# Fourteen second-pass pairs by seven products, every second one, all units kept in DRAM in two parts

## The chip, the cores and the metric

The kernel runs on one core of a Trainium2 chip. The metric is the device time of one execution in microseconds; lower is better. TensorE is called PE here, VectorE DVE, ScalarE ACT, GpSimd POOL and SyncE SP, as in the profile.

## The reference, cut to what matters

Two layers of a decoder trunk on 256 tokens of width 2048, all in float32:

```python
for l in range(2):
    h = rmsnorm(x, attn_norm_g[l])
    proj = h @ w_in[l]                       # 2048 -> 6144
    ...                                      # attention on one half, gated short conv on the other
    x = x + concat([attn, conv]) @ w_out[l]
    hm = rmsnorm(x, mlp_norm_g[l]) @ w_up[l]           # 2048 -> 8192
    x = x + square(relu(hm)) @ w_down[l]               # 8192 -> 2048
```

The change is in the last two lines, the MLP. `square(relu(hm))` is called the hidden units; `w_down` has 8192 rows and 2048 columns.

## The kernel before, in words

**Precision.** Every float32 operand is cut into two parts of a rounded float32 type: the high part is made by ACT (a copy that rounds), the low part by DVE (operand minus high part). A product of two such operands is three matmuls (high by high, high by low, low by high: `TERMS`). For PE a matmul of 128x128 by 128x512 is the unit of work.

**The MLP, `mlp` (L767).** The 8192 hidden units are taken in 32 pairs (`NP`) of two blocks of 128. There are two passes over the pairs.

- The *first pass* (L1015 to L1055) makes the hidden units of pair i by `w_up` (L961) and multiplies those of pair i-2 with the left 1024 columns of `w_down` by a scheme of seven products in place of eight (L1011). For that it needs, beside the four blocks of the units, four sums of them (S1 to S4, L984 to L987), and sums of the weights.
- The *second pass* (L1114 to L1177) multiplies the units with the right 1024 columns of `w_down`. It cannot make the units again, so the first pass has written them to DRAM, and the second pass loads them back. A pair in the tuple `SEVEN` (L36) is done by seven products, 7 x 3 = 21 matmuls (L1117 to L1134); any other pair (`PLAIN`) is done directly, 2 x 4 x 3 = 24 matmuls (L1169 to L1175).

Between the two passes PE does the left columns of pairs 30 and 31 directly (48 matmuls, L1090, called the left rest below). Their units are the last two users of the two `f` buffers.

**What the second pass loads of the units.** Plain pairs come in blocks of two (`block`, L1059): tile `g`, two DMAs of 512 KB on POOL's queue from the DRAM tile `plain`; there are four buffers. Pairs in `SEVEN` are of two kinds. Those in `WHOLE` (every second one) were written as finished forms in two parts (`both`, 896 KB) and are loaded straight into an `f` tile by a DMA on POOL's queue (L907). The others were written as raw units (`hid`, 448 KB), are loaded by a DMA on SP's queue into an `h` tile (L910), and ACT and DVE make the two parts (`rounded`, L1000, 128x896 each). `f` has two buffers, for both passes; a load into one waits until PE has done with what was in it.

**What sets the order.** PE's order is that of the code. `weights.take` makes the forms of weights three jobs ahead, in the order `made_in` (L931 to L945), which places the four jobs of a `SEVEN` pair (three kinds of weight forms and the loading of its units) beside jobs of the plain pairs ahead of it. The other engines' orders are set by a scheduler when the program is built; each engine and each DMA queue then runs its list strictly in order. `w_down` is loaded by SP, 1024 KB for each pair and pass: `draw` tiles for `SEVEN` pairs, `raw` for plain ones (L814).

**In this case.** `SEVEN` is (4, 6, 8, 10, 12, 15, 17, ..., 29), 13 pairs; 6, 10, 15, 19, 23 and 27 are `WHOLE`. The second pass starts with plain pairs 0 to 3, then does pair 4.

Of the kernel before, what the change touches and what calls it, by code (L numbers as in the profile page):

```python
# [9 lines left out]
F32 = mybir.dt.float32  # L10
F32R = mybir.dt.float32r
# [4 lines left out]
P = 128  # L16
# [16 lines left out]
AHEAD = 3  # L33
NP = DFF // (2 * P)
LAG = 2
SEVEN = (4, 6, 8, 10, 12, 15, 17, 19, 21, 23, 25, 27, 29)  # L36
WHOLE = SEVEN[1::2]
PLAIN = tuple(i for i in range(NP) if i not in SEVEN)

OUT_JOBS = D // P // 2 * (D // CH)  # L40
# [68 lines left out]
def trunk(ctx: ExitStack, tc: tile.TileContext, x, w_in, w_out, conv_w, q_norm_g, k_norm_g,  # L109
          lambda_q1, lambda_k1, lambda_q2, lambda_k2, subln_g, attn_norm_g, mlp_norm_g,  # L110
          w_up, w_down, rel_bias, selector, out):
    nc = tc.nc
# [7 lines left out]
    dram = ctx.enter_context(tc.tile_pool(name="dram", bufs=1, space=bass.MemoryType.DRAM))  # L120
# [8 lines left out]
    def behind(*instructions):  # L129

        stack = ExitStack()
        for ins in instructions:
            stack.enter_context(tc.issue_after(ins.ins))
        return stack
# [632 lines left out]
    def mlp(l, mnorm, ahead, last):  # L767
# [3 lines left out]
        with ExitStack() as scope:  # L771
            upool = scope.enter_context(tc.tile_pool(name="upool", bufs=3))
            fpool = scope.enter_context(tc.tile_pool(name="fpool", bufs=2))
            second = scope.enter_context(tc.tile_pool(name="second", bufs=1))
# [3 lines left out]
            def tile_of(tag, shape, dtype, *rooms):  # L778
                n = turn[tag] = turn.get(tag, -1) + 1
                pool, tag_in = rooms[max(n - (tag == "draw"), 0) % len(rooms)]  # L780
                return pool.tile(shape, dtype, tag=tag_in, name=tag, bufs=1)
# [27 lines left out]
            def load_rows(i, col):  # L809
                raw = (upool.tile([P, 2, 2 * CH], F32, tag="uraw", name="raw") if col and i not in SEVEN else  # L810
                       tile_of("draw", [P, 2, 2 * CH], F32, (first, "draw"), (second, "draw1"),
                               (second, "draw2")))
                with behind(*after_load(None if col else EARLY_DOWN.get(i))):
                    nc.sync.dma_start(  # L814
                        raw, w_down[l][i * 2 * P:(i + 1) * 2 * P, col:col + 2 * CH].rearrange(
                            "(k p) c -> p k c", p=P))
                return raw

            def quarters(i, col=0):


                keep = late if i == SEVEN[0] and col else lambda ins: None

# [65 lines left out]
            for i in range(NP - LAG, NP):  # L889
# [3 lines left out]

            hid = {i: dram.tile([P, 7 * P], F32, name=f"hid{l}_{i}") for i in SEVEN
                   if i not in WHOLE}
            both = {i: dram.tile([P, 2, 7, P], F32R, name=f"both{l}_{i}") for i in WHOLE}
            plain = [dram.tile([P, 2, 2, 4, P], F32R, name=f"plain{l}_{b}")
                     for b in range((len(PLAIN) + 1) // 2)]  # L900
            again, g_loads = {}, []

            def load_again(i):
                if i in WHOLE:
                    f = again[i] = fpool.tile([P, 2, 8, P], F32R, tag="f", name="f")
                    with behind(*g_loads[-1:]):
                        nc.gpsimd.dma_start(f[:, :, 1:], both[i])  # L907
                    return
                again[i] = tile_of("h", [P, 8, P], F32, (fpool, "h"), (second, "h"))
                nc.sync.dma_start(again[i][:, 1:].rearrange("p a c -> p (a c)"), hid[i])  # L910

            def unit(i):
                def make():
                    f = again[i] if i in WHOLE else rounded(again[i], 1, 8)
                    later = SEVEN.index(i) + 1
                    if later < len(SEVEN):
                        load_again(SEVEN[later])
                    return f
                return make
# [12 lines left out]
            mine = [where[i] + k for i in PLAIN for k in range(2)]  # L932
            slots = {}
            for i in SEVEN:
                before = [j for j in mine if j < where[i]][-4:] if i != SEVEN[0] else [
                    mine[0], mine[2], mine[5], mine[6]]
                js = [where[i] + k for k in (1, 2, 0, 3)]
                if len(before) == 4 and SEVEN.index(i) and where[SEVEN[SEVEN.index(i) - 1]] > before[0]:
                    before = [before[2], before[2], before[3], before[3]]
                for j, b in zip(js, before):  # L940
                    slots.setdefault(b, []).append(j)
# [32 lines left out]
            def square(i, h):  # L974


                u = h[:, 0:4].rearrange("p a c -> p (a c)")
                nc.scalar.activation(u, u, AF.Relu)
                top = h[:, 0:4].rearrange("p (k t) c -> p k t c", t=2)[:, :, 0]
                nc.vector.tensor_mul(top, top,  # L980
                                     mnorm.ratio.unsqueeze(1).to_broadcast([P, 2, P]))
                nc.scalar.activation(u, u, AF.Square)
                if i < NP - LAG:
                    nc.vector.tensor_add(h[:, S1], h[:, A21], h[:, A22])  # L984
                    nc.vector.tensor_sub(h[:, S2], h[:, S1], h[:, A11])
                    nc.vector.tensor_sub(h[:, S3], h[:, A11], h[:, A21])
                    nc.vector.tensor_sub(h[:, S4], h[:, A12], h[:, S2])  # L987
                if i in hid:
                    nc.gpsimd.dma_start(hid[i], h[:, 1:].rearrange("p a c -> p (a c)"))
                if i in SEVEN:  # L990
                    f = rounded(h, 1, 8)
                    if i in WHOLE:
                        nc.gpsimd.dma_start(both[i], f[:, :, 1:])
                    return f
                f = rounded(h, 0, 8 if i < NP - LAG else 4)
                b = PLAIN.index(i)
                stored.append(nc.gpsimd.dma_start(plain[b // 2][:, b % 2], f[:, :, :4]))
                return f

            def rounded(h, lo, hi):  # L1000
                f = fpool.tile([P, 2, 8, P], F32R, tag="f", name="f")
                nc.scalar.activation(f[:, 0, lo:hi], h[:, lo:hi], AF.Copy)
                nc.vector.tensor_sub(f[:, 1, lo:hi], h[:, lo:hi], f[:, 0, lo:hi].bitcast(F32))
                return f
# [10 lines left out]
            for i in range(NP):  # L1015
                j = i - LAG
                end = i == NP - 1
                h = tile_of("h", [P, 8, P], F32, (fpool, "h"), (second, "h"))
                if i == 0:
                    two = [mm.tile([P, 2, CH], F32, tag="mm2", name=f"up{c}")[:, 0].rearrange(  # L1020
                        "p (h s) -> p h s", h=2) for c in range(2)]
                    for kh in range(2):
                        for c in range(2):
                            up_part(two[c], kh)
                            if kh:
                                evict(two[c], h[:, 2 * c:2 * c + 2])
                    fs[0] = square(0, h)
                    continue
# [85 lines left out]
            for i in range(NP):  # L1114
                if i in SEVEN:
                    f = weights.take()
# [34 lines left out]
                if slot == 1 and b == 0:  # L1151
                    load_again(SEVEN[0])
                if i == PLAIN[-1]:
                    both = [weights.take() for k in range(2)]
# [34 lines left out]
    for l in range(DEPTH):  # L1189
        mnorm, ahead = mixer(l, norm, first_loads if l == 0 else lambda weights: None)  # L1190
        norm = mlp(l, mnorm, ahead, l == DEPTH - 1)
# [32 lines left out]
```

## Time and profile before

| what | value |
|---|---|
| time, median of 3 runs | 2140.8 us (2140.31 to 2140.87) |
| the profiled execution | 2139.43 us |
| its span, first to last instruction | 2137.7 us |
| DVE busy | 1689.8 us (79%) |
| ACT busy | 1292.7 us (60%) |
| moved by DMA | 487.79 MB, mean 228 GB/s |
| SP's queue (q1) | 413.40 MB |
| POOL's queue (q0) | 72.51 MB |
| second pass, layer 0 / layer 1 | from 906.4 us / from 1967.6 us |

The profiled execution is 1.4 us below the median of the runs, and lies 1.7 us over its span. A row of groups reads: line, engine, operation, out<-in by the program's names, shape, count, then busy us, mean ns of one, and idle time before it. Matmuls overlap each other, so the duration of one (389 ns) is not the time that PE spends for each; that is read from how long a run of them takes. DMA rows tell when a DMA was issued; "to landing" is the time from there until its data was in place.

### The profile page before, as it was taken

How to read it: one execution, taken by the hardware profiler on the slowest of the kernel's cores; microseconds unless marked ns; L12 is line 12 of the kernel's file. 1: busy time of each engine (PE TensorE's matmuls, PEld its weight loads, DVE VectorE, ACT ScalarE, POOL GpSimd, SP SyncE). 2: the span in 40 equal slices, each digit the busy share in tenths (PEclk: the TensorE clock that was granted, in tenths of full speed). 3: DMA queues.
4: the chain of work that ended last, by engine and by line, in shares of the span. 5: the costliest groups of instructions: out<-in, count | busy, mean ns of one | idle time of the engine just before them, and what ended most of it. 6: DMA issues, size and time to landing. Idle time of an engine off the chain costs nothing.

```text
span 2137.7 us, 28947 instructions
## 1 busy us (share of the span) xinstructions
PE 2127.5 (100%) x10956; PEld 1809.3 (85%) x10956; DVE 1689.8 (79%) x2307; ACT 1292.7 (60%) x1761; POOL 174.8 (8%) x263
## 2 busy tenths in 40 slices
PE   9999999999999999999999999999999999999999
PEld 7888888888888888888888888888888888888887
DVE  6677656788888888799866776567888888887987
ACT  6566445566666666655565664456666666665553
POOL 1021200000000000100001221000000000001000
PEclk9999999999999999999999999999999999999999
DMA  7655568577777777899466556776777777778992
GB/s 258 188 160 166 183 205 264 182 237 235 233 235 234 241 237 235 258 389 317 150 207 178 160 164 188 219 242 201 226 239 241 227 239 242 232 239 277 392 316 93
DMA packets 291701, 487.79 MB, mean 228 GB/s; under 512 B 10689, under 2 KB 191592, under 8 KB 291560
## 3 DMA queue, kind: packets, MB, share of 16 engines
q1 hardware_dynamic: 266936, 413.40, 61.0%
q0 software_dynamic: 24576, 72.51, 10.2%
q8 instruction: 86, 1.41, 0.3%
q14 instruction: 55, 0.45, 0.1%
q10 hardware_dynamic: 48, 0.02, 0.0%
HBM read 446.42 MB, written 39.48 MB: 227 GB/s over the span
## 4 chain that ended last, share of the span: by engine, by line
PE 97%; DVE 1%; DMA 1%; ACT 0%; issue 0%; SPq 0%; ACTq 0%
PE upc L961 31%; PE pr L1011 14%; PE rt L1173 9%; PE o L397 8%; PE rt L1011 6%; PE ci L419 4%; PE gc L419 4%; PE gb L419 4%; PE v L397 4%; PE k L397 4%; PE q L397 4%; PE upw L961 1%; PE pr L1090 1%; PE up L961 1%; PE sc L595 1%; PE av L634 0%
## 5 line engine op out<-in xcount | busy, mean ns | idle before, releaser
L310 ACT ACTIVATE whi<-raw 128x1024 fp32r<-128x1024 f32 x324 | 343.1, 1060 | 430.6 <-PE rt L1173 104.0
L311 DVE TENSOR_TENSOR wlo<-raw,whi 128x1024 fp32r<-128x1024 f32 x324 | 398.2, 1230 | 244.0 <-ACT whi L310 238.9
L961 PE MATMUL upc<-nT,uhi 128*128 128x512 f32 x1920 | 477.5, 391 | 0.0
L804 ACT ACTIVATE uhi<-uraw 128x1024 fp32r<-128x1024 f32 x256 | 270.5, 1057 | 266.2 <-PE upc L961 239.5
L805 DVE TENSOR_TENSOR ulo<-uraw,uhi 128x1024 fp32r<-128x1024 f32 x256 | 313.1, 1223 | 126.4 <-ACT uhi L804 114.9
L961 PEld LDWEIGHTS upc<-nT,uhi 128*128 128x128 f32 x1920 | 352.8, 188 | 68.1
L961 PEld LDWEIGHTS upc<-nT,ulo 128*128 128x128 f32 x1920 | 261.9, 190 | 18.7
L961 PE MATMUL upc<-nT,ulo 128*128 128x256 f32 x1920 | 267.7, 282 | 0.0
L1173 PE MATMUL rt<-whi,g 128*128 128x512 f32 x576 | 182.1, 389 | 0.0
L397 PE MATMUL o<-whi,cat 128*128 128x512 f32 x512 | 159.5, 390 | 0.0
L1173 PEld LDWEIGHTS rt<-whi,g 128*128 128x128 f32 x576 | 108.2, 188 | 22.3
L397 PEld LDWEIGHTS o<-whi,cat 128*128 128x128 f32 x512 | 96.1, 188 | 19.7
L1173 PE MATMUL rt<-wlo,g 128*128 128x512 f32 x288 | 112.2, 389 | 0.0
L829 DVE TENSOR_TENSOR t13l<-t,t13h 128x1024 fp32r<-128x1024 f32 x86 | 105.1, 1222 | 2.5
L829 DVE TENSOR_TENSOR b2l<-draw,b2h 128x1024 fp32r<-128x1024 f32 x86 | 104.7, 1217 | 0.8 <-ACT b2h L828 0.8
L829 DVE TENSOR_TENSOR t24l<-t,t24h 128x1024 fp32r<-128x1024 f32 x86 | 104.7, 1217 | 0.5 <-ACT t24h L828 0.5
L842 DVE TENSOR_TENSOR t<-draw 128x1024 f32<-128x1024 f32 x86 | 104.8, 1219 | 0.3
L397 PE MATMUL o<-wlo,cat 128*128 128x512 f32 x256 | 99.6, 389 | 0.0
L828 ACT ACTIVATE t13h<-t 128x1024 fp32r<-128x1024 f32 x86 | 91.4, 1063 | 4.3 <-PE rt L1011 1.8
L1011 PE MATMUL pr<-t13h,f 128*128 128x512 f32 x240 | 93.8, 391 | 0.0
L828 ACT ACTIVATE b2h<-draw 128x1024 fp32r<-128x1024 f32 x86 | 90.4, 1051 | 3.4 <-PE rt L1011 2.6
L828 ACT ACTIVATE t24h<-t 128x1024 fp32r<-128x1024 f32 x86 | 90.5, 1052 | 3.3 <-DVE t L846 3.3
(359 smaller groups left out, 3857.4 us busy)
## 6 DMA issues: line engine op xcount, KB each, us to landing
uraw<-in_w_up_dram SPq DMA_DIRECT2D x128, 1024.0 KB, 5.6
raw<-in_w_in_dram SPq DMA_DIRECT2D x190, 512.0 KB, 3.9
draw<-in_w_down_dram SPq DMA_DIRECT2D x90, 1024.0 KB, 7.4
raw<-in_w_down_dram SPq DMA_DIRECT2D x38, 1024.0 KB, 6.6
raw<-in_w_out_dram SPq DMA_DIRECT2D x64, 512.0 KB, 5.4
plain<-f POOLq DMA_DIRECT2D x38, 512.0 KB, 3.7
g<-plain POOLq DMA_DIRECT2D x38, 512.0 KB, 9.3
both<-f POOLq DMA_DIRECT2D x12, 896.0 KB, 4.4
```

The costliest lines, as they stand in the source:

```text
L310: self.splits.append((nc.scalar.activation(hi, raw, AF.Copy), nc.vector.tensor_sub(lo, raw, hi.bitcast(F32))))
L311: nc.vector.tensor_sub(lo, raw, hi.bitcast(F32))))
L397: nc.tensor.matmul(acc[:, t], a.ap[:, pa, k % KG, t * P:(t + 1) * P], (hi, lo)[pw][:, j], start=(k == 0 and n == 0), stop=(k == nk - 1 and ...
L419: nc.tensor.matmul(acc[:, f, 0] if part else acc[:, f], wt[:, k % 4, fs], a.ap[:, 0, k % KG] if part else a.ap[:, :, k % KG], start=(part ...
L804: nc.scalar.activation(hi, src, AF.Copy)
L805: nc.vector.tensor_sub(lo, src, hi.bitcast(F32))
L828: keep(nc.scalar.activation(hi, src, AF.Copy))
L829: keep(nc.vector.tensor_sub(lo, src, hi.bitcast(F32)))
L842: keep(nc.vector.tensor_sub(t[:, 0:2], raw[:, :, 1], raw[:, 0]))
L961: nc.tensor.matmul(acc[:, 0] if part else acc, wt[:, k], a.ap[:, 0, k % KG] if part else a.ap[:, :, k % KG], start=(part == 0 and kh == 0 ...
L1011: nc.tensor.matmul(prods[n], f[:, pa, a], b[pw], start=(start and m == 0), stop=(stop and m == 2))
L1173: nc.tensor.matmul(prods[p], blocks[b][:, slot, pa, 2 * k + t], w[pw][:, n], start=(i == PLAIN[0] and k == 0 and m == 0), stop=False)
```

## The change

`SEVEN` becomes every second pair from 3 to 29, 14 pairs; so plain pairs are 0, 1, 2, 4, 6, ..., 28, 30, 31, 18 in place of 19. `WHOLE` goes: all `SEVEN` pairs are written as forms in two parts (896 KB) and loaded straight into `f` by POOL's queue. The raw units in DRAM (`hid`), their load on SP's queue and the second `rounded` are gone. The jobs of the first `SEVEN` pair are placed beside other plain jobs, since only three plain pairs are ahead of it.

```diff
-SEVEN = (4, 6, 8, 10, 12, 15, 17, 19, 21, 23, 25, 27, 29)
-WHOLE = SEVEN[1::2]
+SEVEN = tuple(range(3, NP - 2, 2))
...
-            hid = {i: dram.tile([P, 7 * P], F32, name=f"hid{l}_{i}") for i in SEVEN
-                   if i not in WHOLE}
-            both = {i: dram.tile([P, 2, 7, P], F32R, name=f"both{l}_{i}") for i in WHOLE}
+            whole = {i: dram.tile([P, 2, 7, P], F32R, name=f"whole{l}_{i}") for i in SEVEN}
...
             def load_again(i):
-                if i in WHOLE:
-                    f = again[i] = fpool.tile([P, 2, 8, P], F32R, tag="f", name="f")
-                    with behind(*g_loads[-1:]):
-                        nc.gpsimd.dma_start(f[:, :, 1:], both[i])
-                    return
-                again[i] = tile_of("h", [P, 8, P], F32, (fpool, "h"), (second, "h"))
-                nc.sync.dma_start(again[i][:, 1:].rearrange("p a c -> p (a c)"), hid[i])
+                f = again[i] = fpool.tile([P, 2, 8, P], F32R, tag="f", name="f")
+                with behind(*g_loads[-1:]):
+                    nc.gpsimd.dma_start(f[:, :, 1:], whole[i])
 
             def unit(i):
                 def make():
-                    f = again[i] if i in WHOLE else rounded(again[i], 1, 8)
+                    f = again[i]
...
                 before = [j for j in mine if j < where[i]][-4:] if i != SEVEN[0] else [
-                    mine[0], mine[2], mine[5], mine[6]]
+                    mine[0], mine[1], mine[3], mine[4]]
...
-                if i in hid:
-                    nc.gpsimd.dma_start(hid[i], h[:, 1:].rearrange("p a c -> p (a c)"))
                 if i in SEVEN:
                     f = rounded(h, 1, 8)
-                    if i in WHOLE:
-                        nc.gpsimd.dma_start(both[i], f[:, :, 1:])
+                    nc.gpsimd.dma_start(whole[i], f[:, :, 1:])
                     return f
```

The first place is POOL's list at the end of the first pass and the start of the second, layer 0, before. `plain0_9` is the store of pair 31's units, the `g` rows are the blocks of plain pairs (x2: two DMAs), the `f` rows the units of a `SEVEN` pair, whose number stands behind `both0_`.

```order
L1062 DMA g_8427<-plain0_0_3766 128x1024 x2
L997 DMA plain0_9_3775<-f_8408 128x2x512
L1062 DMA g_8520<-plain0_1_3767 128x1024 x2
L1062 DMA g_8565<-plain0_2_3768 128x1024 x2
L1062 DMA g_8643<-plain0_3_3769 128x1024 x2
L907 DMA f_8595<-both0_6_3760 128x2x896
L1062 DMA g_8801<-plain0_4_3770 128x1024 x2
L1062 DMA g_8967<-plain0_5_3771 128x1024 x2
L907 DMA f_8823<-both0_10_3761 128x2x896
```

The same place of the change; `whole0_3` are the units of pair 3.

```order
L1052 DMA g_8427<-plain0_0_3767 128x1024 x2
L987 DMA plain0_8_3775<-f_8408 128x2x512
L1052 DMA g_8520<-plain0_1_3768 128x1024 x2
L1052 DMA g_8565<-plain0_2_3769 128x1024 x2
L1052 DMA g_8681<-plain0_3_3770 128x1024 x2
L903 DMA f_8568<-whole0_3_3753 128x2x896
L903 DMA f_8570<-whole0_5_3754 128x2x896
L1052 DMA g_8844<-plain0_4_3771 128x1024 x2
L903 DMA f_8700<-whole0_7_3755 128x2x896
```

The first `f` load stands at the same place in the list, behind one store and the six `g` DMAs of blocks 1 to 3; it is for pair 3 now, where it was for pair 6. Layer 1 reads the same.

The second place is SP's list at the same time, before: `w_down` and the raw units.

```order
L814 DMA raw_8456<-in_w_down_dram 128x2x1024
L814 DMA draw_8474<-in_w_down_dram 128x2x1024
L814 DMA raw_8523<-in_w_down_dram 128x2x1024
L814 DMA raw_8570<-in_w_down_dram 128x2x1024
L910 DMA h_8568<-hid0_4_3753 128x896
L814 DMA draw_8668<-in_w_down_dram 128x2x1024
L910 DMA h_8737<-hid0_8_3754 128x896
L814 DMA draw_8761<-in_w_down_dram 128x2x1024
L910 DMA h_8903<-hid0_12_3755 128x896
L814 DMA raw_8609<-in_w_down_dram 128x2x1024
```

And the change at this place:

```order
L813 DMA raw_8456<-in_w_down_dram 128x2x1024
L813 DMA draw_8474<-in_w_down_dram 128x2x1024
L813 DMA raw_8543<-in_w_down_dram 128x2x1024
L813 DMA raw_8572<-in_w_down_dram 128x2x1024
L813 DMA draw_8628<-in_w_down_dram 128x2x1024
L813 DMA draw_8724<-in_w_down_dram 128x2x1024
L813 DMA raw_8610<-in_w_down_dram 128x2x1024
L813 DMA raw_8706<-in_w_down_dram 128x2x1024
L813 DMA draw_8804<-in_w_down_dram 128x2x1024
```

The three loads of raw units (448 KB each) are gone from between the weights; the loads of weights stand in the same order otherwise (three `raw`, one `draw` among them, then two `draw`, then the fourth `raw`, which is that of pair 3 before and of pair 4 now).

The third place is PE, where pair 3 stands in layer 0. Before, after the last matmul of pair 2:

```order
L1173 MATMUL rt08_8519<-wlo_8589,g_8520 128x512
L1173 MATMUL rt08_8519<-whi_8588,g_8520 128x512
L1173 MATMUL rt02_8516<-whi_8611,g_8520 128x512
L1173 MATMUL rt02_8516<-wlo_8612,g_8520 128x512
L1173 MATMUL rt02_8516<-whi_8611,g_8520 128x512
```

And now:

```order
L1163 MATMUL rt08_8519<-wlo_8607,g_8520 128x512
L1163 MATMUL rt08_8519<-whi_8606,g_8520 128x512
L1001 MATMUL rt01_8658<-b1h_8476,f_8568 128x512
L1001 MATMUL rt01_8658<-b1l_8477,f_8568 128x512
L1001 MATMUL rt01_8658<-b1h_8476,f_8568 128x512
```

Right behind pair 2, where PE went on with `g`, it now reads `f_8568`, the tile that the first `f` load on POOL's queue fills.

## The prediction

> **What bounds the kernel now.** I read the page first (busy shares, the chain that ended last), then PE's waits, then the chain and the DMA rows of the second pass.
>
> ```profile
> PE 2127.5 (100%) x10956; PEld 1809.3 (85%) x10956; DVE 1689.8 (79%) x2307; ACT 1292.7 (60%) x1761; POOL 174.8 (8%) x263
> PE 97%; DVE 1%; DMA 1%; ACT 0%; issue 0%; SPq 0%; ACTq 0%
> PE up L961 <- DVE nT L277: 2.5, 4, 0.7
> PE q L397 <- DVE wlo L331: 1.5, 2, 1.3
> ```
>
> PE is the bound: it is busy in all but 10 us of the span, the chain is PE for 97%, and its two longest sums of waits are 2.5 and 1.5 us, neither of them in a second pass. So a matmul less is time gained, work taken from DVE or ACT gains nothing, and a new wait of PE costs its full length. The chain in the second pass, of layer 0 and then of layer 1:
>
> ```profile
> 895.63 10.88 PE pr L1090 x48
> 906.51 21.76 PE rt L1173 x96
> 928.27 4.76 PE rt L1011 x21
> 933.03 5.44 PE rt L1173 x24
> ```
> ```profile
> 1967.79 21.89 PE rt L1173 x96
> 1989.69 4.76 PE rt L1011 x21
> ```
>
> The columns are start, duration, matmuls. 96 matmuls take 21.76 us, so one costs PE 0.2267 us. Pairs 0 to 3 are those 96; the first pair by seven products, pair 4, begins at 928.27. Pair 3 therefore begins at 928.27 - 5.44 = 922.8 in layer 0 and at 1967.79 + 72 x 0.2267 = 1984.1 in layer 1. These are the moments when the changed PE first needs a loaded `f`.
>
> What serves it is POOL's queue. Its issues in layer 0, then the one `f` load in layer 1, and how long after their issue the six `g` loads (first) and the `f` loads (layer 0, layer 1) landed:
>
> ```profile
> 899.67 0.71 POOL L997 DMA_DIRECT2D plain<-f  x1 [7.96 <-DVE f L1003]
> 900.38 3.20 POOL L1062 DMA_DIRECT2D g<-plain  x6
> 906.81 0.71 POOL L907 DMA_DIRECT2D f<-both  x1 [3.23 <-PE pr L1090]
> 917.70 1.07 POOL L1062 DMA_DIRECT2D g<-plain  x2 [10.18 <-PE rt L1173]
> ...
> 1968.09 0.71 POOL L907 DMA_DIRECT2D f<-both  x1 [3.22 <-PE pr L1090]
> ```
> ```profile
> DMA to landing us min/median/max: 8.2/13.4/19.9
> DMA to landing us min/median/max: 20.9/20.9/20.9
> DMA to landing us min/median/max: 21.1/21.1/21.1
> ```
>
> The `f` load landed at 906.81 + 20.9 = 927.7 in layer 0 and at 1968.09 + 21.1 = 1989.2 in layer 1. The last of the six `g` loads was issued at about 903.0 and landed 19.9 later, at 922.9; the `f` load came 4.8 us behind it. So the queue is served in order, and this load waits for what stands ahead of it, not for its own issue. How fast the queue moves:
>
> ```profile
> 898.00:902.00 4.00, 4.00 (x19) 3.34 (x18) 3.20 (x5) 2.71 (x4) 2.33 (x5) 1.00 0.39 94
> 902.00:908.00 6.00, 6.00 (x28) 4.95 (x28) 5.80 (x7) 4.49 (x6) 2.29 (x4) 1.00 1.07 346
> 908.00:926.00 18.00, 18.00 (x81) 14.93 (x80) 14.69 (x16) 8.29 (x9) 1.07 (x2) 1.00 1.08 401
> ```
> ```profile
> q1 hardware_dynamic: 966, 3.63, 53.8%
> q0 software_dynamic: 997, 3.57, 53.5%
> ```
>
> The last three columns of the windows are the granted clock, the DMA share and GB/s: from 908 to 926 the DMA engines are full at 401 GB/s. In that window SP's queue (q1) moved 3.63 MB and POOL's (q0) 3.57 MB: each gets half, 200 GB/s, as long as both have work.
>
> **The change part by part.**
>
> *Six matmuls less.* Fourteen pairs in place of 13 take 21 matmuls in place of 24; that is 3 for each layer, 6 in all, 6 x 0.2267 = 1.36 us gained on PE.
>
> *The units of pair 3.* In the changed order POOL's first `f` load is for pair 3 and stands behind the same store and the same six `g` loads. Its buffer is free sooner (it takes that of pair 30, used until the middle of the left rest, 895.63 + 5.4 = 901), so it is issued at about 903.5 and not 906.8, but it lands when the queue has served what is ahead. If the queue moves as before, that is 927.7 and 1989.2, and PE, which needs it at 922.8 and 1984.1, waits 4.9 and 5.1 us: 10.0 us. Everything on PE stands behind it, since its order is fixed. What can make it shorter is less traffic on SP's queue:
>
> ```profile
> 899.40 0.34 SPq L910 DMA_DIRECT2D h<-hid  x1
> 900.74 0.37 SPq L814 DMA_DIRECT2D draw<-in_w_down_dram  x1
> 906.19 0.34 SPq L910 DMA_DIRECT2D h<-hid  x1
> 907.99 9.75 SPq L814 DMA_DIRECT2D raw<-in_w_down_dram  x3
> ```
> ```profile
> h<-hid SPq DMA_DIRECT2D x14, 448.0 KB, 4.3
> f<-both POOLq DMA_DIRECT2D x12, 896.0 KB, 8.1
> ```
>
> The two `hid` loads go, 2 x 0.459 = 0.92 MB, which took 0.92 / 0.401 = 2.3 us of full DMA. If SP's queue then stood empty for as long, POOL's load would land 2.3 us sooner and the waits would be 2.6 and 2.8 us, 5.4 in all. If the weight loads behind close up, nothing is won and it stays at 10.0. They can close up only in part: the next `draw` is issued at 900.74 and needs about 5 to 6 us at half rate, to some 907; the fourth `raw` waits for DVE to be done with the first one (907.99 before, perhaps 1.5 us sooner without the rounding of pair 4's units), and the window from 898 to 902 (94 GB/s, though DMAs were issued from 899.4 on) shows that a DMA moves little for a microsecond or two after its issue. I take an empty queue of about 1 us in each layer, nearer to closing up: waits of 3.9 and 4.1 us, **8.0 us**.
>
> *What is late next.* Pair 5's `f` is next in the queue: 0.92 MB at 200 GB/s, 4.6 us behind pair 3's, against the 10.2 us (4.76 + 5.44) that PE is busy before it needs it. Pair 7's is issued when PE has done pair 3, behind two `g` loads (1.05 MB, 5.2 us); it lands some 10 us behind pair 5's at the latest, about 15 us after pair 3 starts, and is needed 20.4 us after. From there each `f` load may start when the `SEVEN` pair two before is done, and is needed 5.44 + 4.76 + 5.44 = 15.6 us later; such loads landed after 8.1 us (median). So only pair 3 waits. If this cover failed, each us late would cost 26 us (13 pairs, two layers).
>
> *DVE and ACT.* DVE's groups in the second pass of layer 0:
>
> ```profile
> L311 DVE TENSOR_TENSOR wlo<-raw,whi 128x1024 fp32r<-128x1024 f32 x36 | 43.9, 1222 | 14.9 <-ACT whi L310 14.6
> L829 DVE TENSOR_TENSOR t24l<-t,t24h 128x1024 fp32r<-128x1024 f32 x13 | 15.8, 1218 | 0.0
> L846 DVE TENSOR_TENSOR t<-draw,t 128x512 f32<-128x512 f32 x13 | 8.9, 688 | 0.2
> L1003 DVE TENSOR_TENSOR f<-h,f 128x896 fp32r<-128x896 f32 x7 | 7.6, 1084 | 0.0
> ```
>
> A plain pair costs DVE 2 x 1.22 = 2.4 us, a `SEVEN` pair four such operations of 1.22 and three of 0.69, 6.9 us. One pair more by seven adds 4.5 us for each layer, the seven roundings gone take 7.6 us off. DVE has less to do, and PE waited for none of it worth naming: nothing either way. The forms of pair 3's weights come early enough, because their loads stand where those of pair 4 stood, while PE needs them 5.4 us sooner and DVE has the rounding less. If that failed, it would hide inside the wait for `f`.
>
> *The first pass.* Seven raw stores of 448 KB become 896 KB, and one plain store of 512 KB does, in each layer: 0.46 MB, or 1.1 us of full DMA, in pairs that take about 16 us.
>
> ```profile
> 423.00:443.00 20.00, 20.00 (x105) 17.16 (x104) 17.70 (x26) 14.70 (x19) 0.72 (x1) 1.00 0.84 261
> both<-f POOLq DMA_DIRECT2D x12, 896.0 KB, 4.4
> ```
>
> The DMA engines are 0.84 busy there, and the twelve pairs that already store 896 KB made PE wait for nothing. Zero; 8 x 1.1 us for each layer if that spare time were gone.
>
> *Sum.* Profiled execution 2139.43 - 1.36 + 8.0 = 2146.1. It lies 1.4 us below the median of the runs, so on that scale **2147.4 us**, 0.3% slower. This measurement can tell about 0.2%, 4.3 us, from no change. Ends of the unknown wait (5.4 and 10.0): 2144.8 and 2149.4.
>
> [...] In every window quoted the granted clock is 1.00, and PE's longest wait is 1.3 us, so the trace shows no long stop and what follows one. [...]
>
> [...]
>
> **The rivals.**
>
> 1. *PE's clock falls in the stop.* The price from rows: at half clock a `SEVEN` pair of 4.76 us takes 4.76 us more; half a pair slowed in each layer is 2 x 2.4 = 4.8 us on top, 2152.2; a whole pair each, 2157. For it: the waits of about 4 us are longer than anything in the trace. Against: nothing in the trace.
> 2. *Not slower: pair 3's `f` lands in time.* This decides if the load lands before 922.8. With SP's queue idle, the 0.52 + 6 x 0.52 + 0.92 = 4.6 MB would need 11.4 us at 401 GB/s and be there by 914. For it: `f` loads later in the pass land in 8.1 us. Against: SP's list still has four weight loads there, and six `g` loads land ahead in both layers. Then 2140.8 - 1.4 = 2139.4.
> 3. *Every `f` load is late.* All of them compete on POOL's queue now, 0.92 + 0.52 MB in 10.2 us, 141 GB/s, under its half of 200. One us late each: 2147 + 26 = 2173. Against: the 15.6 us above.
> 4. *The change does not do what it says.* PE's list holds exactly six matmuls less, so no.
>
> **How the numbers follow.** Forecast (a wait before pair 3 in both layers, clock kept) 0.62; rival 1 0.20; rival 2 0.12; rival 3 and other mishaps 0.06. The range leaves out rival 2 (0.12), rival 3 and the upper end of rival 1: 2142.5 to 2153.5; its lower end lets each wait be about 1 us under the bound of 2.6 to 2.8. Faster by over 0.2%, under 2136.5, has no mechanism: 0.02. Within 0.2%: rival 2 and the low end of the forecast, 0.19. Slower: 0.79.
>
> **What would show it.** In the trace after: PE idle before the first matmul with `f` behind pair 2, about 4 us, in both layers, ended by the DMA `f<-whole`; that load landing near 926.7 and 1988.2; no PE idle before pairs 5, 7 and later; 0.2267 us for each matmul after the wait (rival 1: 0.45 for a few us, and a granted clock under 1). PE without any idle there would make the prediction wrong, as would a wait for DVE instead of the DMA.

## The result, and the profile after

The changed kernel takes 2147.4 us (median of 6 runs, 2146.22 to 2150.45) against 2140.84 us (6 runs, 2139.36 to 2141.69): ratio 1.0033 [1.0021, 1.0046], slower. The profiled execution took 2148.12 us, its span is 2146.3 us, 8.6 us more than before.

The page after, busy times and the chain that ended last:

```profile
PE 2129.6 (99%) x10950; PEld 1810.0 (84%) x10950; DVE 1690.8 (79%) x2303; ACT 1287.1 (60%) x1751; POOL 186.5 (9%) x277
PE 94%; DMA 3%; DVE 1%; issue 1%; ACT 0%; POOL 0%; SPq 0%; ACTq 0%; POOLq 0%
```

PE runs the six matmuls less, and yet it is busy for 2.1 us more, so some of its matmuls have become slower. DMA, 1% of the chain before, is 3%. The longest sums of PE's waits after (us in total, times, longest):

```profile
PE rt L1001 <- DMA f<-whole: 4.6, 2, 2.3
PE up L954 <- DVE nT L276: 2.6, 4, 0.7
PE rt L1148 <- DVE x L1057: 2.3, 1, 2.3
```

The first is the forecast wait for pair 3's `f`, in both layers, but 2.3 us each and not 4. The third stands at the end of layer 0; the same wait before:

```profile
PE rt L1158 <- DVE x L1067: 0.4, 1, 0.4
```

Where the 8.6 us arise is seen in the chain of after, in both layers (start, duration, matmuls):

```profile
903.46 21.62 DMA f<-whole
...
925.12 5.07 PE rt L1001 x21
930.20 5.44 PE rt L1163 x24
...
1062.82 8.20 DMA raw<-in_w_in_dram
...
1071.13 1.07 ACT whi L309
...
1072.22 0.76 DVE wlo L310
...
1073.36 0.76 DVE x L1057
...
1074.16 4.60 PE rt L1148 x12
...
1080.51 4.55 PE q L396 x20
...
1970.31 21.55 DMA f<-whole
...
1991.90 6.66 PE rt L1001 x21
1998.57 5.44 PE rt L1163 x24
```

The end of layer 0 in the chain before:

```profile
1070.28 3.02 PE rt L1158 x12
...
1075.05 9.99 PE q L397 x44
```

Setting the same moments of the two chains side by side gives an account of the difference:

| moment | before | after | later by | new since the moment above |
|---|---|---|---|---|
| pair 3 done, layer 0 | 928.27 | 930.20 | 1.93 | -0.68 (three matmuls), 2.6 (wait for `f` and restart) |
| first matmul after the stop at the end of layer 0 | 1070.28 | 1074.16 | 3.88 | 1.95 (wait 2.3 in place of 0.4) |
| first `q` of layer 1 | 1075.05 | 1080.51 | 5.46 | 1.58 (12 matmuls in 4.60, not 3.02) |
| pair 3 done, layer 1 | 1989.69 | 1998.57 | 8.88 | -0.68, 4.1 (wait for `f`, then 6.66 for 21 matmuls, not 5.07) |
| span | 2137.7 | 2146.3 | 8.6 | -0.3 |

What makes the 12 and the 21 matmuls slow is the granted clock. The windows of after; the third number from the end is the clock, then DMA share and GB/s:

```profile
898.00:902.00 4.00, 4.00 (x20) 3.30 (x19) 3.15 (x5) 2.71 (x4) 2.38 (x5) 1.00 0.43 141
...
908.00:926.00 18.00, 15.66 (x70) 12.65 (x69) 15.00 (x16) 7.33 (x7) 1.10 (x2) 1.00 1.08 403
...
925.00:928.40 3.40, 3.28 (x14) 2.73 (x15) 1.36 (x2) 2.28 (x3) 0.00 (x0) 1.00 1.09 406
...
1074.30:1077.70 3.40, 3.40 (x9) 2.63 (x10) 1.95 (x4) 1.33 (x4) 0.00 (x0) 0.50 0.97 358
1992.50:1995.90 3.40, 3.40 (x10) 2.66 (x9) 1.89 (x2) 1.82 (x3) 0.00 (x0) 0.50 1.08 407
1996.00:1999.00 3.00, 3.00 (x15) 2.46 (x14) 1.90 (x2) 2.48 (x3) 0.12 (x1) 1.00 1.08 403
```

After the stop at the layer's end and after the one in layer 1, PE runs at half clock for 3.4 us, then at full clock again. After the equally long stop in layer 0, at 925, it keeps its clock. The clock record of the trace shows a difference between them: the two slow stretches begin at 1074.32 and 1992.51 and last 3.413 us each, and their beginnings lie 269 times this length apart. Counted back in steps of 3.413 us, this grid has lines at 1989.10, 1070.91, 924.14 and 920.73. Each of the two stops that cost the clock lies within one step, with 2.3 us of idle PE in it; the stop in layer 0, from 922.78 to 925.12, is parted by the line at 924.14 into 1.4 and 0.98 us.

The loads that the two kinds of stop go back to, first `g` and `f`. The landing times of the six `g` loads, and of pair 3's `f` (the same in both layers):

```profile
DMA to landing us min/median/max: 7.0/12.8/17.3
DMA to landing us min/median/max: 21.6/21.6/21.6
```

POOL's first loads, and SP's list at the same time:

```profile
900.32 3.20 POOL L1052 DMA_DIRECT2D g<-plain  x6
903.46 0.71 POOL L903 DMA_DIRECT2D f<-whole  x1
...
900.69 0.37 SPq L813 DMA_DIRECT2D draw<-in_w_down_dram  x1
906.28 6.41 SPq L813 DMA_DIRECT2D raw<-in_w_down_dram  x2
```

POOL issues its first six `g` at the same time as before (900.3, 900.4 before), yet the last lands after 17.3 us and not 19.9, and `f` at 903.46 + 21.6 = 925.1, 2.6 us sooner than the 927.7 of before. The store and the first `g` no longer meet a `hid` load: from 898 to 902 the DMA engines move 141 GB/s, 94 before. SP issues nothing between the `draw` at 900.69 and the next `raw` at 906.28, which came at 907.99 before.

At the end of layer 0 the two loads of layer 1's bias (`rev`, 1024 KB each, POOL) meet the first weights (`raw`, SP). After:

```profile
1062.03 1.81 POOL L261 DMA_DIRECT2D rev<-by_dist_d  x2 [18.62 <-PE rt L1001]
...
1062.82 11.02 SPq L349 DMA_DIRECT2D raw<-in_w_in_dram  x5
```

Before:

```profile
1061.18 1.82 POOL L262 DMA_DIRECT2D rev<-by_dist_d  x2 [29.88 <-PE rt L1011]
...
1060.90 9.05 SPq L350 DMA_DIRECT2D raw<-in_w_in_dram  x5
```

Before, the weights were 0.3 us ahead; after, the bias is 0.8 us ahead, and the weights on the chain need 8.2 us. ACT rounds them at 1071.13, DVE makes their low part, and behind that on DVE's list stands the operation on `x` (L1057) for which PE waits: the fourth to seventh rows of the chain above.

### The profile page after: what moved, and what is told of

The parts are those of the page before. It is cut to its first block, busy times and chain, and to the rows that moved or that the text cites. A ratio compares the mean times of both kernels' runs of the same rounds, so it can differ in the third digit from the quotient of the medians.

```text
span 2146.3 us, 28874 instructions
## 1 busy us (share of the span) xinstructions
PE 2129.6 (99%) x10950; PEld 1810.0 (84%) x10950; DVE 1690.8 (79%) x2303; ACT 1287.1 (60%) x1751; POOL 186.5 (9%) x277
## 4 chain that ended last, share of the span: by engine, by line
PE 94%; DMA 3%; DVE 1%; issue 1%; ACT 0%; POOL 0%; SPq 0%; ACTq 0%; POOLq 0%
PE upc L954 31%; PE pr L1001 13%; PE o L396 8%; PE rt L1163 7%; PE rt L1001 6%; PE ci L418 4%; PE gc L418 4%; PE gb L418 4%; PE v L396 4%; PE k L396 4%; PE q L396 3%; DMA f<-whole 2%; PE upw L954 1%; PE up L954 1%; DMA raw<-in_w_in_dram 1%
## 5 line engine op out<-in xcount | busy, mean ns | idle before, releaser
L310 DVE TENSOR_TENSOR wlo<-raw,whi 128x1024 fp32r<-128x1024 f32 x320 | 393.5, 1231 | 235.4 <-ACT whi L309 229.7
L1163 PE MATMUL rt<-whi,g 128*128 128x512 f32 x544 | 172.7, 389 | 0.0
L1163 PEld LDWEIGHTS rt<-whi,g 128*128 128x128 f32 x544 | 102.1, 188 | 21.2
L1163 PE MATMUL rt<-wlo,g 128*128 128x512 f32 x272 | 105.8, 389 | 0.0
L827 ACT ACTIVATE b2h<-draw 128x1024 fp32r<-128x1024 f32 x88 | 92.7, 1054 | 11.9 <-PE rt L1001 11.0
```

The lines of the kernel that those rows point to most:

```text
L310: nc.vector.tensor_sub(lo, raw, hi.bitcast(F32))))
L827: keep(nc.scalar.activation(hi, src, AF.Copy))
L1163: nc.tensor.matmul(prods[p], blocks[b][:, slot, pa, 2 * k + t], w[pw][:, n], start=(i == PLAIN[0] and k == 0 and m == 0), stop=False)
```

## The experiments

The theory from these traces: two separate causes. POOL's list puts `f` behind six `g` loads (pair 3's wait); fourteen pairs in place of thirteen change which buffer comes free last, and so who is first at the end of layer 0. The rival to the first: the extra bytes of the forms load the DMA engines, wherever they stand. The rival to the second: the stop at the layer's end is a consequence of the late `f`.

**Pair 3's `f` ahead of the `g` loads.**

```diff
...
                 if slot == 0 and b == 0:
                     with tc.issue_after(stored[-1].ins):
+                        ahead_of = load_again(SEVEN[0])
+                    with tc.issue_after(ahead_of.ins):
                         block(1)
                 if slot == 1 and b + 2 < len(plain):
-                    block(b + 2)
-                if slot == 1 and b == 0:
-                    load_again(SEVEN[0])
+                    with behind(*g_loads[-1:]):
+                        block(b + 2)
```

> The changed kernel, with the load of pair 3's units moved ahead of the six loads of blocks 1 to 3 on POOL's queue. If the queue's order is the cause of the two waits of 2.3 us for f, both go: the load lands by about 908 us in layer 0 (one store and itself, 1.4 MB, from 901 on), the half clock that followed the wait in layer 1 (1.7 us) goes too, and the time falls from 2147.4 to about 2141. What is left over is the wait of 2.3 us at the end of layer 0 and its half clock. If instead the larger volume of forms (14 MB more through DMA) or DVE is the cause, the time stays at 2147 and PE waits elsewhere.

Measured: 2141.36 us (11 runs, 2140.07 to 2143.08) against 2139.58, ratio 1.0007 [0.9998, 1.0016]. Its load of `f`, and its chain there:

```profile
DMA to landing us min/median/max: 8.8/8.8/8.8
```

```profile
906.26 16.32 PE rt L1164 x72
922.58 4.76 PE rt L1001 x21
```

The same bytes on the same DMA engines land after 8.8 us and not 21.6, and pair 3 follows pair 2 without a gap. So the place in POOL's list is the cause, not the bytes. The stop at the layer's end is untouched (2.3 us, then half clock from 1072.0), so it does not come from the late `f`. Seven of the 11 runs have a mean clock of 0.999 and take 2141.1 to 2143.1, four have 1.000 and take 2140.1 to 2140.4: the half clock comes in some executions only.

**All units in two parts, the old thirteen pairs.** The kernel before with `WHOLE = SEVEN`:

```diff
-WHOLE = SEVEN[1::2]
+WHOLE = SEVEN
```

> The kernel before with one part of the change alone: all 13 pairs stored and loaded in two parts, the old pairs (first one is pair 4). Pair 4 starts 5.4 us later than pair 3, and the load of its units lands at about 925 us in layer 0, 3 us before PE needs it at 928. So by the queue's order PE does not wait for f and the time is 2140 to 2142 (above 2141 if the bias loads get ahead at the layer's end). If storing and loading in two parts is itself the cost, it is 2145 or more, and PE waits at pair 4.

Measured: 2139.63 us (11 runs) against 2139.58, ratio 1.0000 [0.9991, 1.0009]. The beginning of pair 4 in its chain:

```profile
929.31 4.76 PE rt L1011 x21
```

No stop, PE goes on at full pace: here the first `f` is for pair 4, which begins one plain pair (5.4 us) later than pair 3. It was issued at 904.55 and landed at most 23.2 us later, at 927.8, 1.5 us before PE took it at 929.3. The larger stores and loads cost nothing by themselves, and no stop at the layer's end came with them (0.4 us).

**A longer wait.** One unused copy of 512 KB in DRAM ahead of pair 3's `f` on POOL's queue:

```diff
                 with behind(*g_loads[-1:]):
+                    if i == SEVEN[0]:
+                        g_loads.append(nc.gpsimd.dma_start(spare_d, plain[0][:, 0]))
+                with behind(*g_loads[-1:]):
                     nc.gpsimd.dma_start(f[:, :, 1:], whole[i])
```

> The changed kernel with one more DMA of 512 KB (DRAM to DRAM, not used) ahead of pair 3's units on POOL's queue. By the queue's order these land later by at least 2.6 us (0.52 MB at half of 401 GB/s), so PE waits 4.9 us or more in each layer. If the half clock comes with a long enough stop of PE, it now follows the wait in both layers, not in one, for 3.4 us each; with the wait at the end of layer 0 that is 2147.4 + 2 x 2.6 + 1.7 = 2154 or more. If the load does not wait for what is ahead of it, the time stays at 2147.

Measured: 2157.11 us (4 runs, 2154.91 to 2158.78) against 2139.45, ratio 1.0080 [1.0064, 1.0095]. Its waits for `f`, and the windows around the end of the one in layer 0 and of the one in layer 1:

```profile
PE rt L1005 <- DMA f<-whole: 11.9, 2, 6.1
```

```profile
927.70:934.50 6.80, 5.86 (x14) 4.60 (x15) 2.45 (x3) 2.63 (x3) 0.00 (x0) 0.50 1.08 407
1999.50:2006.30 6.80, 4.50 (x11) 3.55 (x12) 1.90 (x2) 1.83 (x3) 0.00 (x0) 0.50 1.08 406
```

That is 11.9 - 4.6 = 7.3 us more of waiting, and after each of the two stops a half clock that lasts 6.8 us, not the 3.4 that were expected. PE works 5.86 and 4.50 us of them, so 2.9 and 2.3 us are lost there. Of the 9.7 us between this median and that of the change (2157.11 - 2147.4; different runs of the kernel before, 2139.45 and 2140.84) the waits are the largest part. In the profiled execution the clock fell after both stops of about 6 us, and after the one of 2.4 us at the layer's end.

**The pairs alone.** The kernel before with the fourteen new pairs; every second one still comes by raw units and SP, pair 3 among them:

```diff
-SEVEN = (4, 6, 8, 10, 12, 15, 17, 19, 21, 23, 25, 27, 29)
+SEVEN = tuple(range(3, NP - 2, 2))
 WHOLE = SEVEN[1::2]
...
-                    mine[0], mine[2], mine[5], mine[6]]
+                    mine[0], mine[1], mine[3], mine[4]]
```

> The other part of the change alone: the 14 new pairs, but every second one (3, 7, 11, ...) still as raw units on SP's queue, as in the kernel before. Pair 3 is one of these, so by the queue's order PE does not wait for its units. With 14 pairs the bias loads still get ahead at the end of layer 0, so the wait of 2.3 us and its half clock stay: 0 to 2.5 us over the kernel before. If pair 3 by seven products comes too early for DVE or for the weights, PE waits for DVE at pair 3 and it is 4 us or more over it.

Measured: 2145.11 us (8 runs, 2143.53 to 2146.51) against 2139.45, ratio 1.0027 [1.0016, 1.0037]. Its longest wait, the loads at the layer's end, and the window behind the stop:

```profile
PE rt L1158 <- DVE x L1067: 3.7, 1, 3.7
```

```profile
1059.21 1.82 POOL L262 DMA_DIRECT2D rev<-by_dist_d  x2 [18.33 <-PE rt L1011]
...
1060.30 2.94 SPq L350 DMA_DIRECT2D raw<-in_w_in_dram  x4
```

```profile
1072.30:1079.10 6.80, 6.05 (x16) 4.79 (x17) 3.41 (x7) 2.87 (x6) 0.00 (x0) 0.50 0.43 145
```

No wait for `f` at all, as expected, since pair 3's units come by SP's queue. But the bias is 1.1 us ahead of the weights, the stop at the layer's end is 3.7 us, and the clock is halved for 6.8 us after it. The sum from these, -1.36 + (3.7 - 0.4) + half of the 6.05 us that PE worked at half clock, is 5.0, beside 5.7 measured. This is more than was expected, and it shows that the stop belongs to the fourteen pairs, not to the two-part units.

**The bias held back, with a new tile.** POOL copies one column of the first weights into a small new tile, and the bias loads are ordered behind that copy:

```diff
+            with behind(*([weights.probe] if weights.probe else ())):
+                nc.gpsimd.dma_start(
+                    rev, bass.AP(src.tensor, src.offset, [[1, P], [REL, NH], [1, S]]))
...
+                        seen = small.tile([P, 1], F32, tag="seen", name="seen", bufs=1)
+                        self.probe = nc.gpsimd.tensor_copy(seen, raw[:, 0, 0:1])
```

> The changed kernel, with the two bias loads of layer 1 held on POOL until the first weights of layer 1 have landed (a one-column copy on POOL reads them). If the wait of 2.3 us of PE near 1072 us comes from the bias loads getting ahead of those weights on the DMA engines, it falls to 0.4 us or less as before, the half clock behind it (1.7 us) goes, and the time falls by 2 to 3.7 us to about 2144; the waits for f stay at 2.3 us in each layer. If the wait comes from the shift of the second pass itself, it stays, and the time is 2147.

Measured: 2153.22 us (5 runs, 2151.54 to 2156.2) against 2139.58, ratio 1.0067 [1.0054, 1.0080]: a miss. The stop at the layer's end is 0.4 us, as wanted, but the waits for `f` are 5.9 us in place of 4.6, which was not followed up, and the kernel is some 6 us slower than the change, far more than these 1.3 us. The same edit together with `f` ahead of the `g` loads:

> Both edits together. If the two waits and their half clocks make up all of the loss, only the six matmuls less are left: 2140.8 - 1.4 = 2139.4, a little under the kernel before, granted clock 1.000. If a general cost of the change remains (more bytes, POOL's issues), it is above 2141.

Measured: 2146.9 us (5 runs, 2146.49 to 2147.87) against 2139.58, ratio 1.0036 [1.0023, 1.0048]: a miss too, with neither of the two stops left and a clock of 1.000. So something other than waits and clock costs it. Its chain in the output projection of layer 0:

```profile
303.02 25.19 PE o L401 x108
```

The same work in the kernel before:

```profile
302.46 24.51 PE o L397 x108
```

Each of 108 matmuls takes 25.19 / 108 = 0.2332 us and not 0.2269, without any wait.

**The tile alone.** The kernel before with a tile of 4 bytes for each partition that nothing reads:

```diff
+    unused = small.tile([P, 1], F32, tag="seen", name="seen", bufs=1)
+    nc.gpsimd.memset(unused, 0.0)
```

> The kernel before with nothing but one more tile of 4 bytes in each partition in the pool of small tiles (set to zero, never read), which moves the tiles behind it. If the slower matmuls of the second and third run come from where the tiles lie, the matmuls of the output projection take 0.232 us in place of 0.227 and the time is about 5 us over the kernel before; if they came from the copy on POOL, there is no difference.

Measured: 2148.6 us (4 runs, 2148.15 to 2149.64) against 2139.45, ratio 1.0044 [1.0030, 1.0058], 9.15 us slower where about 5 were expected, at a clock of 1.000. Its output projection in the chain:

```profile
302.91 25.19 PE o L399 x108
```

It has the same slow matmuls. The 768 of the output projection in both layers make up 768 x 0.0063 = 4.8 us; where the rest of the 9.15 us arises was not followed up. That it comes from where the tiles behind the new one lie, the reading of the expectation, is not shown: by how much they move and which operand it is was not tried, and this run also adds the instruction that zeroes the tile. So the two misses say nothing against the theory of the bias.

**Both repairs without a new tile.** The copy goes into a tile that is there already:

```diff
...
+                        self.probe = nc.gpsimd.tensor_copy(sel[0:1, 0:1], raw[0:1, 0, 0:1])
```

> The two edits of the third run again, but the copy on POOL writes into a tile that is there already, so that no tile in SBUF moves. If the 32 bytes of the new tile were what slowed the matmuls from 0.227 to 0.233 us, they are at 0.227 again, PE waits neither for f nor near 1070 us, the clock stays at 1.000 and the time is 1.4 us under the kernel before run beside it. If the copy or the later bias loads cost the 6 us, it is 5 us or more over it.

Measured: 2137.91 us (11 runs, 2137.54 to 2138.52) against 2139.45 (18 runs, 2138.8 to 2139.95), ratio 0.9994 [0.9985, 1.0002]. The interval holds 1, but every one of the 11 runs is below every one of the 18. At the layer's end:

```profile
PE rt L1154 <- DVE x L1062: 0.4, 1, 0.4
```

```profile
1066.54 1.82 POOL L262 DMA_DIRECT2D rev<-by_dist_d  x2
...
1060.24 2.39 SPq L351 DMA_DIRECT2D raw<-in_w_in_dram  x4
```

With both stops gone, what is left is -1.54 us, beside the 1.36 us of the six matmuls. This is the fastest of the kernels here, 9.0 us below the one whose copy goes into a new tile. That a new tile takes 32 bytes, as the expectation has it, no run shows; it is declared with 4 for each partition.

**The bias held back alone**, with the copy into the existing tile and `f` where the change has it:

> The changed kernel with the bias loads of layer 1 held back as in the fifth run, without a new tile, and pair 3's units where the change has them. Only the waits for f are left: 2 x 2.3 us less the six matmuls (1.4 us) is 3.2 us over the kernel before, and up to 1.7 us more for each of them that halves the clock: 3 to 7 us. If the waits for f were a consequence of the wait at the layer's end, they would be gone.

Measured: 2146.49 us (7 runs, 2142.89 to 2147.77) against 2139.48, ratio 1.0030 [1.0019, 1.0041], 7.0 us over it, at the upper end of what was expected. The stop at the layer's end is 0.4 us; the waits for `f` are 2.65 and 2.71 us, 5.4 in all, and in the profiled execution each was followed by 3.4 us of half clock. The run with a mean clock of 1.000 took 2142.89, those with 0.998 took 2146.49 to 2147.77. So a stop of 2.3 to 2.7 us cost its own length here, or 1.7 us more (half of the 3.4 us at half clock), and that differed from one execution to the next.

**Which buffer comes free last.** `f` ahead of the `g` loads, and the turn of the two buffers of the weight forms `t24` begun with the other one, so that after fourteen pairs it ends as after thirteen:

```diff
...
-            turn = {}
+            turn = {"t24h": 0, "t24l": 0}
...
```

> The kernel of the first run (pair 3's units ahead), with the two buffers of the forms t24 taken in the other turn, so that the last pair's t24 lies where it lay with 13 pairs. If the bias loads of layer 1 get ahead because the buffer below them is now free before the last pair is done (14 pairs turn the two buffers once more), they are issued again after the first weights of layer 1, PE's wait near 1070 us is 0.4 us, the clock stays at 1.000 and the time is 1.5 us under the kernel before. If the turn of that buffer has nothing to do with it, the wait of 2.3 us and its half clock stay and it is 1 to 2 us over the kernel before.

Measured: 2141.96 us (11 runs, 2139.74 to 2144.61) against 2139.48, ratio 1.0013 [1.0004, 1.0022]. The loads at the layer's end:

```profile
1062.94 1.82 POOL L261 DMA_DIRECT2D rev<-by_dist_d  x2 [19.96 <-PE rt L1001]
...
1062.39 2.24 SPq L349 DMA_DIRECT2D raw<-in_w_in_dram  x4
```

PE's longest sum of waits, and the window behind a part of it:

```profile
PE up L954 <- DVE nT L276: 4.2, 6, 1.1
```

```profile
402.10:405.50 3.40, 3.07 (x11) 2.46 (x12) 2.67 (x5) 2.79 (x4) 0.00 (x0) 0.50 0.93 328
```

The weights are ahead of the bias again, by 0.55 us, and the stop is 0.4 us: the turn of the buffer is the cause. The time did not fall as in the kernel with both repairs, because the other turn moved work at the start of the first pass: PE's waits for `nT` rise from 2.6 to 4.2 us, and stops of 1.1 and 0.6 us close together, at 400 to 402 us, were followed by half clock there. With PE at work in 3.07 us of it, -1.36 + (4.2 - 2.6) + half of 3.07 is 1.8, beside 2.5 measured. Why the turn lengthens these waits was not followed up.

## Why the prediction was right, point by point

The time and the direction came out as forecast, and the forecast wait is there, in both layers and for the reason given. But it is only about half of the loss. Without the 1.36 us gained, the profiled execution lost 10.0 us: about 5 by the waits for `f` and the restarts behind them, 1.95 by the stop at the end of layer 0, which the prediction did not have, and 3.2 by the clock, which it had as a rival. The number agrees to the tenth, and that is chance: errors cancel.

- *Six matmuls less, -1.36 us.* Right: 10956 became 10950, and with the stops removed 1.54 us were gained.
- *PE waits for pair 3's `f`, in both layers, and for no later pair's.* Right: two waits, both ended by the DMA `f<-whole`; none before pairs 5, 7 and later. The load landed at 925.1 and 1991.9, where the text has 926.7 and 1988.2; the second is late because PE was already 5.5 us late at the start of layer 1. The cause is the place in POOL's list, as the first experiment shows (landing after 8.8 us from the front of the list, 21.6 us from its end): the six `g` loads ahead of it made up 12.8 us, its own issue 0.71.
- *8.0 us for these waits.* This term failed: 4.6 us measured, under the lower bound of 5.4. The step is "I take an empty queue of about 1 us in each layer, nearer to closing up". The weight loads closed up too little. `f` landed 2.6 us sooner, all of the 2.3 us that the two `hid` loads had taken of the DMA engines and a little more. The fourth `raw` came 1.7 us sooner, near the 1.5 that the text allowed, and still did not fill what `hid` had left; SP had nothing to issue for 5 us, while POOL's queue had work all the time.
- *The first pass, DVE and ACT: nothing.* Right up to pair 3: PE ended pair 2 at 925.12 - 2.34 = 922.8 in layer 0, the moment of before. PE's one longer wait for DVE, at the end of layer 0, goes back to weights that landed late.
- *What is late next.* Incomplete. The text looked as far as the end of the second pass and no further. The fourteenth pair turns the buffers of `t24`, so the bias loads of layer 1 start ahead of its first weights, and PE stops for 2.3 us at the end of layer 0: 1.95 us that no step had.
- *Rival 1, the clock.* The forecast had "clock kept". In the profiled execution it was not kept, and none of the six runs of the change has a mean clock of 1.000: four have 0.999 and two 0.998, which fits one place or two with 3.4 us at half clock. So the rival happened beside the forecast, not in place of it, and after stops of 2.3 us, where the text thought of 4. It cost about 1.6 us at each of two places in the profiled execution. The rival's own price (half a pair to a whole pair slowed, 2.4 to 4.8 us for each stop) was too high for these, since the half clock lasted 3.4 us; after the stops of 3.7 to 6.1 us in two of the experiments 2.3 to 3.0 us were lost, near its lower end. That PE's clock halves after a stop, on which this price rests, no row quoted in the prediction shows; in the profiled execution of the change it was 0.50 for 3.4 us after two of its three stops of 2.3 us.
- *Rivals 2, 3 and 4.* Refuted: the load was late, no other was, and the instructions were as the text says.

So there were 8.0 - 4.6 = 3.4 us too much for the waits, and 1.95 + 3.2 = 5.1 us missing for the layer's end and the clock. The profiled execution, 2148.12 us, is accordingly 2.0 us above the sum of 2146.1 that was made for it; the median of the runs, most of them at a mean clock of 0.999 where the profiled one has 0.998, falls on the forecast. That is the other half of the chance: the forecast added 1.4 us because the profiled execution before lay under the median of its runs, and the profiled execution of the change lies 0.7 us above the median of its own.

## What to carry to other kernels

Before a load is moved to another queue, add up what stands ahead of it there and set its landing against the moment when it is needed; here the same bytes from the front of the list landed after 8.8 us in place of 21.6 and made PE wait for nothing. When a buffer that is used in turns gets one user more, look at which loads start after the last of them, at the end of the stage and beyond it. A stop of a saturated PE is to be priced at its length plus the clock: here 1.7 us in part of the executions after stops of 2.3 to 2.7 us, and 2.3 to 3.0 us in the profiled executions after stops of 3.7 to 6.1 us.

## What the runs showed of the hardware that was not expected

- The granted clock was 0.50 for 3.4 us after stops of 2.3 us (two of the three in the profiled execution of the change, one in that of the first experiment), and after stops of 1.11 and 0.57 us close together in the run with the other turn of the buffers. After stops of 3.73 us (the pairs alone) and of 6.15 and 5.78 us (the longer wait) it was 0.50 for 6.8 us in the profiled executions.
- In the clock record of the change the two slow stretches behind its stops last 3.413 us each, and a third begins at 2146.11 and is cut off by the end of the execution; they begin 269 and 45 steps of 3.413 us apart. Cut into such steps, its profiled execution has 2.32 and 2.29 us of idle PE in the two steps ahead of these two stretches, and 1.36 us or less in every other step up to PE's last matmul. In that of the kernel before it is 1.33 us or less in every step up to the last matmul, and the one stretch at half clock begins at 2136.96, behind it. So a stop of 2.3 us that fell into one step cost the clock, and one of the same length that a line of the grid parted did not. The stretches of 6.8 us (the pairs alone, the longer wait) had 0.75, 0.94 and 2.30 us of idle PE in them (6.05, 5.86 and 4.50 us busy of 6.80), those of 3.4 us 0.33 us or less (3.07 us busy of 3.40 in the run with the other turn, all 3.40 in the change and the first experiment). Where the grid lay in the executions without a profile is not on record.
- With a tile of 4 bytes a partition more, placed ahead of others and set to zero, 128x512 matmuls of the output projection started every 0.2332 us in place of 0.2269 (108 in 25.19 us, not 24.51), and the kernel was 9.15 us slower, at a clock of 1.000 and with less than 1 us more of waits.
- Of two queues, the one that started first by less than 1 us was served first in both profiled executions. Before, with the weights 0.3 us ahead, only SP's of the two moved data from 1063 to 1065 (0.72 MB). After, with the bias 0.8 us ahead, only POOL's did from 1062 to 1065 (0.27 MB), and it had 0.41 of the 0.59 MB of the next 2 us; the first weights needed 8.2 us, and PE's stop rose from 0.4 to 2.3 us.
